# Routing the last two token tiles of a mixture-of-experts block: VectorE's steps in a hand-written order, and unread products on TensorE

## The chip, the cores and the metric

The kernel runs on one core of a Trainium2 chip. The metric is the device time of one execution in microseconds (us), as the median of several runs. A profile of one execution shows when each instruction of the five engines ran: TensorE (PE, with its weight loads as PEld), VectorE (DVE), ScalarE (ACT), GpSimd (POOL) and SyncE (SP, which issues transfers).

## What is computed

One layer of a streaming encoder for 1024 tokens of width 1024: a token mixer (attention and pooling branches, gated, then a projection `w_out`), a layer norm, and a mixture of experts with two-stage routing.

```
x = layer_norm(ALPHA * x + mix, ln1_gain, ln1_bias)
g_prob = softmax(x2 @ w_router_group + b_router_group)      # 4 groups
g_p, g_idx = top_k(g_prob, 1)
e_logit = (x2 @ w_router_expert + b_router_expert)          # 8 experts of the chosen group
e_p, e_local = top_k(softmax(e_logit), 2)
weights = g_p * e_p / sum(e_p)
...
yb = (silu(gate) * up) @ w_down[e]        # for the tokens of each of 32 experts
out = segment_sum(yb * row_w, row_tok)
x = layer_norm(ALPHA * x + ffn, ln2_gain, ln2_bias)
```

## The kernel before

Tokens are worked in eight tiles of 128 behind the mixer. The projection by `w_out` goes in groups of tiles, (0, 1), 2, 3, 4, 5 and (6, 7). For each tile `residual` adds the input and `norm` does the layer norm (L788 to L798), and then the tile goes through five steps, called by `step`:

- `turn` (L813, L814): TensorE transposes the tile x in two groups of four pieces, and ScalarE copies each group into the tile xT.
- `y` (L949): ScalarE writes ALPHA times x, which POOL stores.
- `route`: `logits` multiplies xT by the router's weights (L820, 16 products of 36 columns with their weight loads), VectorE adds the bias (L822, tile lg), and then some twenty small VectorE instructions of 4 or 32 columns (L829 to L857) pick the group G, the first and the second expert (oh), their masks M, and the sum of the masks, Ms. ScalarE has one exponential in it (L832).
- `weights` (L865 to L874): the two weights of the token. VectorE forms the negative of the first maximum (L869), ScalarE takes an exponential (L870), and VectorE makes the weights of it.
- `places` (L879 to L891): TensorE counts with `tri`, `one` and the running count `cum` how many earlier tokens chose the same expert, and VectorE makes one-hot rows (tile ohr) out of it by comparing (L890).
- `place` (L898, L899): TensorE multiplies the one-hot rows, which puts tokens and weights into the table `first`; VectorE adds it, and L903 and L905 make the entries of an overflow table.

While later tiles are projected, the steps of the earlier ones run beside them. Tiles 6 and 7 have nothing beside them: the list `S5_END` names their steps in order, behind the last projection. When the last `place` is done, `rows_at` (L1017, L1018) turns `first` into row numbers, POOL gathers the rows of the first experts (L1093), TensorE transposes them (L1033, tile X), ScalarE and VectorE split them in two parts (L147, L148), and the first expert's products begin (tile gu, three products L162, L163, L164 for each piece). 32 experts follow.

In the stage before the experts, PE and ACT carry out their instructions in the order of the program text, within a stretch that a `manual_schedule` context marks; VectorE's order is chosen by a scheduler, from estimated times. Each engine works its queue strictly in order, so an instruction that waits holds up all behind it.

Of the kernel before, what the change touches and what calls it, by code (L numbers as in the profile page):

```python
# [11 lines left out]
F32 = mybir.dt.float32  # L12
F32R = mybir.dt.float32r
BF = mybir.dt.bfloat16
# [11 lines left out]
NE = 32  # L26

CAP = 96
# [35 lines left out]
    5: ((3, "places", 3), (10, "turn", 4), (10, "place", 3), (12, "route", 4)),  # L64
    7: ((3, "places", 4), (10, "turn", 5), (10, "place", 4), (12, "route", 5), (21, "places", 5), (26, "place", 5)) + S5_LATE,
}
S5_END = (("y", 6), ("logits", 6), ("route", 6), ("turn", 7), ("y", 7), ("weights", 6), ("logits", 7), ("route", 7), ("places", 6), ("weights", 7), ("place", 6), ("places", 7), ("place", 7))
Y_OUT = (6, 7)
COMB = ()
M4 = 4  # L70
# [36 lines left out]
def body(tc, ctx, A, out):  # L107
# [26 lines left out]
    def st(shape, name="st", dt=F32):  # L134
        return sm.tile([128] + shape, dt, name=nm(name), tag="st", bufs=8)
# [4 lines left out]
    def tiny(shape, name, dt=F32, bufs=2):  # L140
        return (ph["S2"] if "S2" in ph else sm).tile([128] + shape, dt, name=nm(name), tag="t_" + name, bufs=bufs)
# [675 lines left out]
    def logits(xT1):  # L817
        pr = p5.tile([128, 512], F32, name=nm("pr"), tag="R", bufs=2)
        for k in range(8):
            PE.matmul(pr[:, :36], xT1[:, k], wr[:, k], start=k == 0, stop=k == 7)  # L820
        lg = tiny([36], "lg")
        DVE.tensor_add(lg, pr[:, :36], br)  # L822
        return lg, pr

    def route(j, lg, pr):

        s = tiny([16], "s")
        gm, ngm, sg = (s[:, i:i + 1] for i in range(3))
        DVE.tensor_reduce(gm, lg[:, 0:4], AX.X, OP.max)  # L829
        DVE.tensor_scalar(ngm, gm, -1.0, None, op0=OP.mult)  # L830
        eg, G = tiny([4], "eg"), tiny([4], "G")
        ACT.activation(eg, lg[:, 0:4], AF.Exp, bias=ngm, accum_out=sg)  # L832

        le, to = lg[:, 4:36].rearrange("p (g e) -> p g e", g=4), lambda v: v[:, :, None].to_broadcast([128, 4, 8])
        mx, f, oh, t = tiny([2, 4], "mx"), tiny([2, 4], "f"), tiny([2, 4, 8], "oh"), tiny([2, 4, 8], "t", bufs=1)
        tg, fg = tiny([4], "tg"), tiny([1], "fg")
        DVE.tensor_reduce(mx[:, 0], le, AX.X, OP.max)
        DVE.scalar_tensor_tensor(tg, lg[:, 0:4], gm, down8[:, :4], op0=OP.is_equal, op1=OP.mult)
        for k in range(2):
            v = t[:, k]  # L840
            DVE.tensor_tensor(v, le, to(mx[:, k]), op=OP.is_equal)
            DVE.tensor_mul(v, v, down8[:, None, :].to_broadcast([128, 4, 8]))
            if k == 0:
                DVE.tensor_reduce(fg, tg, AX.X, OP.max)
                DVE.tensor_scalar(G, tg, fg, None, op0=OP.is_equal)
            DVE.tensor_reduce(f[:, k], v, AX.X, OP.max)
            DVE.tensor_tensor(oh[:, k], v, to(f[:, k]), op=OP.is_equal)
            if k == 0:
                big = tiny([4, 8], "big", bufs=1)
                DVE.scalar_tensor_tensor(big, oh[:, 0], NEG, le, op0=OP.mult, op1=OP.add)  # L850
                le = big
                DVE.tensor_reduce(mx[:, 1], le, AX.X, OP.max)
        M = tiny([2, NE], "M")
        for k in range(2):
            DVE.tensor_tensor(M[:, k].rearrange("p (g e) -> p g e", g=4), to(G), oh[:, k], op=OP.mult)
        Ms = tiny([NE], "Ms", BF)
        DVE.tensor_add(Ms, M[:, 0], M[:, 1])  # L857
        return M, Ms, pr, s, mx, G, eg

    def weights(j, s, mx, G, eg):  # L860

        gm, ngm, sg, me, gp, m1, m2, nm1, e2, w = (s[:, i:i + 1] for i in range(10))
        eq = tiny([2, 4], "eq", bufs=1)
        for k, m in enumerate((m1, m2)):
            DVE.scalar_tensor_tensor(eq[:, k], mx[:, k], 1.0, G, op0=OP.mult, op1=OP.mult, accum_out=m)  # L865
        DVE.tensor_reduce(me, eg, AX.X, OP.max)
        DVE.reciprocal(sg, sg)
        DVE.tensor_mul(gp, me, sg)
        DVE.tensor_scalar(nm1, m1, -1.0, None, op0=OP.mult)  # L869
        ACT.activation(e2, m2, AF.Exp, bias=nm1)  # L870
        DVE.tensor_scalar(w, e2, 1.0, None, op0=OP.add)
        DVE.reciprocal(w, w)
        DVE.tensor_mul(pay[:, j, 0, 2:3], w, gp)
        DVE.tensor_mul(pay[:, j, 1, 2:3], pay[:, j, 0, 2:3], e2)  # L874

    def places(j, M, Ms, pr):

        pp = pr[:, 256:288]
        PE.matmul(pp, tri, Ms, start=True, stop=False)  # L879
        PE.matmul(pp, one, cum, start=False, stop=True)  # L880
        oh = st([2, CAP + 2 * NE], "ohr")
        at = tiny([2], "at")
        for k in range(2):
            DVE.tensor_scalar(oh[:, k, CAP:CAP + NE], M[:, k], pay[:, j, 0, 3:4], None, op0=OP.mult)
            DVE.tensor_scalar(oh[:, k, CAP + NE:], M[:, k], pay[:, j, k, 2:3], None, op0=OP.mult)
        for k in range(2):
            t = tiny([NE], "pt", bufs=1)
            DVE.scalar_tensor_tensor(t, M[:, k], 1.0, pp, op0=OP.mult, op1=OP.mult, accum_out=at[:, k:k + 1])
        for k in range(2):
            DVE.tensor_scalar(oh[:, k, :CAP], slots, at[:, k:k + 1], None, op0=OP.is_equal)  # L890
        DVE.tensor_add(cum, cum, Ms)  # L891
        return M, pr, oh, at

    def place(j, M, pr, oh, at):

        pf = pr[:CAP, 384:448]
        for k in range(2):
            PE.matmul(pf, oh[:, k, :CAP], oh[:, k, CAP:], start=k == 0, stop=k == 1)  # L898
        DVE.tensor_add(first, first, pf.rearrange("p (c e) -> p c e", c=2))  # L899
        sf = tiny([2], "sf")  # L900
        for k in range(2):
            t = tiny([NE], "pt", bufs=1)
            DVE.scalar_tensor_tensor(t, M[:, k], float(ROWS), cst[:, C_IOTA:C_IOTA + NE], op0=OP.mult, op1=OP.mult,  # L903
                                     accum_out=sf[:, k:k + 1])
        DVE.tensor_add(entry[:, j], sf, at)  # L905

    def store_rows(j):
        for k in range(2):
            q = POOL.indirect_dma_start(out=TAB, out_offset=IO(ap=entry[:, j, k:k + 1], axis=0), in_=pay[:, j, k], in_offset=None,
                                        bounds_check=NE * ROWS - 1, oob_is_err=False)  # L910
            for o in scat:
                tc.declare_no_dep(q.ins, o.ins, reason="other rows of the table")
            scat.append(q)
# [25 lines left out]
    def step(what, j):  # L939

        if what == "turn":
            x = tl[j]["x"]
            tl[j]["t"] = turned(x)
            if j not in Y_OUT:
                POOL.tensor_scalar(x, x, ALPHA, None, op0=OP.mult)
                POOL.dma_start(Y[j * 128:j * 128 + 128], x)
        elif what == "y":
            y = slot2([D], F32, "yy")
            ACT.activation(y, tl[j]["x"], AF.Copy, scale=ALPHA)  # L949
            POOL.dma_start(Y[j * 128:j * 128 + 128], y)  # L950
        elif what == "route":
            if "l" not in tl[j]:
                tl[j]["l"] = logits(tl[j]["t"])
            tl[j]["m"] = route(j, *tl[j]["l"])
            if j < 6:
                weights(j, *tl[j]["m"][3:])
        elif what == "logits":
            tl[j]["l"] = logits(tl[j]["t"])
        elif what == "weights":
            weights(j, *tl[j]["m"][3:])  # L960
        elif what == "places":
            tl[j]["p"] = places(j, *tl[j]["m"][:3])
        else:
            place(j, *tl[j]["p"])
            if j < 6:
                store_rows(j)


    with tc.manual_schedule(engines={mybir.EngineType.PE, mybir.EngineType.Activation}):
        for group in ((0, 1), (2,), (3,), (4,), (5,), (6, 7)):  # L970
            for j in group:
                begin(j)
            todo = list(S5[group[-1]])
            i = 0
            for n in range(2):
                for j in group:
                    for k in range(8):
                        while todo and todo[0][0] <= i:
                            step(*todo.pop(0)[1:])
                        mix(j, k, n)  # L980
                        i += 1
                    if i == 32:
                        for s_ in todo:
                            step(*s_[1:])
                    residual(j, n)
                    if n:
                        norm(j)
        for what, j in S5_END:
            step(what, j)
    ps5.__exit__(None, None, None)  # L990
    s2.__exit__(None, None, None)
    smp.__exit__(None, None, None)
# [427 lines left out]
```

## Time and profile before

| what | value |
|---|---|
| median of 3 runs | 1561.75 us (1561.41 to 1564.54) |
| profiled execution, own time | 1562.51 us |
| its span, first to last instruction | 1560.7 us |
| TensorE busy | 1486.8 us, 95% of the span |
| VectorE busy | 1192.4 us, 76% |
| ScalarE busy | 947.6 us, 61% |
| last projection product starts, first expert product starts | 922.48 us, 947.18 us |

Times in rows of the trace are counted from the start of the span. In a timeline row stand start, duration, engine, line, operation, the tiles written and read, and in brackets how long the engine was idle just before and what ended the wait. Instructions of an engine overlap a little, so distances of starts say more than durations.

### The profile page before, as it was taken

What the parts mean: (1) busy time and instruction counts of PE and PEld (TensorE: products, weight loads), DVE (VectorE), ACT (ScalarE), POOL (GpSimd) and SP (SyncE); (2) the same over time, 40 slices, a digit from 0 to 9 for tenths busy, and PEclk for the clock granted to TensorE, in tenths of its full rate; (3) what the DMA queues carried; (4) which work ended last, traced back from release to release, by engine and by line L of the source; (5) the groups of instructions that cost most, each with busy time, mean ns of one, the idle gap of its engine ahead of it and who ended that gap; (6) DMA issues with size and microseconds to landing.
All of it is one profiled execution on the core that took longest, in us unless ns stands there. A gap on an engine that the chain in (4) does not pass through costs nothing.

```text
span 1560.7 us, 22003 instructions
## 1 busy us (share of the span) xinstructions
PE 1486.8 (95%) x7627; PEld 1188.4 (76%) x7627; DVE 1192.4 (76%) x2284; ACT 947.6 (61%) x1573; POOL 270.3 (17%) x229
## 2 busy tenths in 40 slices
PE   8999999999999999999999988999999999999980
PEld 6988887798798898888887875777777777776750
DVE  5774214987988987775565778999989999898967
ACT  4323124665666666775341126888888888888864
POOL 0001000220211211100002524222222222211410
PEclk9999999999999999999999998999999999999995
DMA  7156223746856755628465577999999999999945
GB/s 237 58 173 202 81 74 102 222 150 169 229 189 175 215 182 145 155 68 303 149 255 209 180 264 267 384 374 376 375 379 358 363 366 358 358 354 371 397 140 215
DMA packets 116977, 375.46 MB, mean 241 GB/s; under 512 B 13767, under 2 KB 44871, under 8 KB 91504
## 3 DMA queue, kind: packets, MB, share of 16 engines
q1 hardware_dynamic: 76128, 303.25, 52.9%
q0 software_dynamic: 40160, 69.96, 17.2%
q8 instruction: 61, 1.00, 0.3%
q10 hardware_dynamic: 576, 0.83, 0.2%
q14 instruction: 52, 0.43, 0.1%
HBM read 312.44 MB, written 69.78 MB: 245 GB/s over the span
## 4 chain that ended last, share of the span: by engine, by line
PE 55%; issue 28%; POOL 9%; DVE 5%; ACT 2%; DMA 1%; POOLq 0%; DVEq 0%; SPq 0%; ACTq 0%
POOL Y L1105 7%; PE ps L570 4%; PE pg L162 4%; PE pg L163 4%; PE pg L164 4%; PE po L621 3%; PE pv L162 2%; PE pv L164 2%; PE pv L163 2%; POOL xg L1093 2%; PE pa L164 2%; PE pa L163 2%; PE pa L162 2%; PE tp L606 2%; PE pw L162 2%
## 5 line engine op out<-in xcount | busy, mean ns | idle before, releaser
L148 DVE TENSOR_TENSOR wh<-we,wh 128x1024 fp32r<-128x1024 f32 x384 | 459.8, 1219 | 52.8 <-ACT wh L147 49.3
L147 ACT CAST wh<-we 128x1024 fp32r<-128x1024 f32 x384 | 400.6, 1047 | 88.5 <-PE gu L164 50.9
L162 PE MATMUL gu<-wh,xT 128*96 128x512 f32 x512 | 203.8, 398 | 0.0
L164 PE MATMUL gu<-wh,xT 128*96 128x512 f32 x512 | 202.2, 395 | 0.5 <-DVE xT L148 0.5
L163 PE MATMUL gu<-wh,xT 128*96 128x512 f32 x512 | 201.3, 393 | 0.0
L1105 POOL DMA_INDIRECT Y<-y,idx x32 | 108.7, 3398 | 265.1 <-ACT y L1113 260.3
L148 DVE TENSOR_TENSOR w<-wraw,w 128x512 fp32r<-128x512 f32 x111 | 75.7, 686 | 93.3 <-ACT w L147 92.9
L147 ACT CAST w<-wraw 128x512 fp32r<-128x512 f32 x111 | 68.5, 621 | 116.0 <-PE pg L164 36.4
L573 ACT ACTIVATE P<-ps,stat 128x256 f32<-128x256 f32 (+7 forms) x128 | 94.9, 742 | 59.0 <-DVE stat L572 58.6
L164 PEld LDWEIGHTS gu<-wh,xT 128*96 128x96 f32 x512 | 82.7, 162 | 36.8 <-DVE xT L148 1.1
L163 PEld LDWEIGHTS gu<-wh,xT 128*96 128x96 f32 x512 | 83.1, 162 | 33.9
L162 PEld LDWEIGHTS gu<-wh,xT 128*96 128x96 f32 x512 | 82.8, 162 | 33.0 <-ACT xT L147 0.2
L162 PE MATMUL dn<-wh,hT 128*96 128x512 f32 x256 | 102.4, 400 | 0.6 <-ACT hT L147 0.6
L570 PE MATMUL ps<-K,Q 128*128 128x512 f32 (+2 forms) x384 | 99.6, 364 | 1.2 <-DVE z L461 0.8
L164 PE MATMUL dn<-wh,hT 128*96 128x512 f32 x256 | 100.7, 393 | 0.0
L163 PE MATMUL dn<-wh,hT 128*96 128x512 f32 x256 | 100.6, 393 | 0.0
L162 PE MATMUL pg<-xT,w 128*128 128x512 f32 x256 | 100.4, 392 | 0.0
L163 PE MATMUL pg<-xT,w 128*128 128x512 f32 x256 | 100.0, 391 | 0.0
L164 PE MATMUL pg<-xT,w 128*128 128x512 f32 x256 | 99.9, 390 | 0.0
L572 DVE TENSOR_REDUCE stat<-ps 128x1 f32<-128x256 f32 (+7 forms) x128 | 95.4, 747 | 1.1
L570 PEld LDWEIGHTS ps<-K,Q 128*128 128x128 f32 x384 | 64.6, 189 | 10.8 <-DVE z L461 1.3
L162 PE MATMUL pv<-w,xT 128*128 128x256 f32 x256 | 72.8, 284 | 0.0
(277 smaller groups left out, 3382.4 us busy)
## 6 DMA issues: line engine op xcount, KB each, us to landing
we<-in_we_dram SPq DMA_DIRECT2D x192, 1024.0 KB, 22.8
wraw<-in_w_dram SPq DMA_DIRECT2D x61, 512.0 KB, 3.8
Q<-RQ POOLq DMA_DIRECT2D x64, 256.0 KB, 5.2
RQ<-rh SPq DMA_DIRECT2D x32, 256.0 KB, 3.3
K<-RK POOLq DMA_DIRECT2D x16, 512.0 KB, 5.2
V<-RV POOLq DMA_DIRECT2D x16, 512.0 KB, 5.5
OT<-ohl SPq DMA_DIRECT2D x48, 128.0 KB, 2.6
oT<-OT POOLq DMA_DIRECT2D x6, 1024.0 KB, 11.6
```

Of the source, the lines that this page charges most:

```text
L147: ACT.copy(hi, src)
L148: DVE.tensor_sub(lo, src, r(hi))
L162: PE.matmul(ps, a[0], b[0], start=start, stop=False)
L163: PE.matmul(ps, a[0], b[1], start=False, stop=False)
L164: PE.matmul(ps, a[1], b[0], start=False, stop=stop)
L570: PE.matmul(ps[:, c:c + n], q[:, o, m, qc], Kt[h, m][:, c:c + n], start=o == 0, stop=o == 1)
L572: DVE.tensor_reduce(st_[:, m:m + 1], ps[:, :W], AX.X, OP.max, negate=True)
L573: ACT.activation(Pt[h, i][m][:, :W], ps[:, :W], AF.Exp, bias=st_[:, m:m + 1], accum_out=st_[:, 2 + m:3 + m])
L606: PE.transpose(ps[:, k], p[:, (4 * g + k) * 128:(4 * g + k) * 128 + 128], ident)
L621: PE.matmul(o[:, 0, c], Vt[h][:, a, kt], aT[kt // 4][:, kt % 4, b, c], start=j == 0, stop=j == len(parts) - 1)
L1093: q = POOL.indirect_dma_start(out=x, out_offset=None, in_=X1, in_offset=IO(ap=idx[:, int(e < NXG), expert[e]:expert[e] + 1], axis=0), boun ...
L1105: q = POOL.indirect_dma_start(out=Y, out_offset=IO(ap=idx[:, 0, expert[e]:expert[e] + 1], axis=0), in_=y, in_offset=None, bounds_check=T - ...
```

## The change

The list `S5_END` goes, and a function `last_two` takes its place, in a context in which VectorE's order too is that of the program text. To write that order, `route`, `weights`, `places` and the new `onehots` and `entries` become generators: each `yield` ends a single VectorE step, and `some`, `by_turns` and `all_of` run so many steps of one, alternate two, or run all. Within `weights`, the negative (now L882) and the exponential (L883) come before the reciprocals. `place` is split into TensorE's part and VectorE's (`placed`). `idle(n)` issues n products of the constants `one` and `tri` (128 x 128, bf16) into a PSUM tile that nobody reads. For the six earlier tiles the same functions run without interleaving. Removed lines of the generators that only moved are left out here.

```diff
-S5_END = (("y", 6), ("logits", 6), ("route", 6), ("turn", 7), ("y", 7), ("weights", 6), ("logits", 7), ("route", 7), ("places", 6), ("weights", 7), ("place", 6), ("places", 7), ("place", 7))
...
+    def all_of(*steps):
+        for g in steps:
+            for _ in g:
+                pass
+
+    def by_turns(g, h):
+
+        for _ in h:
+            next(g, None)
+
+    def some(g, n):
+        for _ in range(n):
+            next(g, None)
...
+    def idle(n):
+
+        ps = p5.tile([128, 512], F32, name=nm("pw"), tag="W", bufs=4)
+        for i in range(n):
+            PE.matmul(ps[:, :128], one, tri, start=True, stop=True)
+
+    def last_two():
+
+        step("y", 6)
+        tl[6]["l"] = logits(tl[6]["t"])
+        r = route(6)
+        some(r, 12)
+        by_turns(r, weights(6))
+        all_of(r)
+        idle(32)
+        step("turn", 7)
+        step("y", 7)
+        all_of(onehots(6, 0), onehots(6, 1))
+        tl[7]["l"] = logits(tl[7]["t"])
+        r = route(7)
+        some(r, 2)
+        by_turns(r, places(6))
+        idle(16)
+        place(6)
+        idle(20)
+        by_turns(r, entries(6))
+        some(r, 2)
+        w = weights(7)
+        for _ in range(7):
+            some(w, 1)
+            some(r, 1)
+        all_of(r)
+        p = places(7)
+        placed(6)
+        all_of(onehots(7, 0), w, onehots(7, 1), p)
+        idle(18)
+        place(7)
+        all_of(entries(7))
+        placed(7)
+        idle(96)
...
-        for what, j in S5_END:
-            step(what, j)
+    with tc.manual_schedule(engines={mybir.EngineType.PE, mybir.EngineType.Activation, mybir.EngineType.DVE}):
+        last_two()
```

The first place where instructions move is VectorE's queue at the logits of tile 7. Tiles with numbers from 9393 to 9423 are those of tile 6 here, lg_9462 and what is made of it belong to tile 7. Before:

```order
L842 TENSOR_TENSOR t_9402<-t_9402,cst 128x32
L846 TENSOR_REDUCE f_9400<-t_9402 128x4
L822 TENSOR_TENSOR lg_9462<-pr_9453,br 128x36
L847 TENSOR_TENSOR oh_9401<-t_9402,f_9400 128x32
L829 TENSOR_REDUCE s_9464<-lg_9462 128x1
L837 TENSOR_REDUCE mx_9470<-lg_9462 128x4
L855 TENSOR_TENSOR M_9420<-G_9397,oh_9401 128x32
L830 TENSOR_SCALAR s_9464<-s_9464 128x1
L838 SCALAR_TENSOR_TENSOR tg_9474<-lg_9462,s_9464,cst 128x4
L857 TENSOR_TENSOR Ms_9423<-M_9420 128x32
L871 TENSOR_SCALAR s_9393<-s_9393 128x1
```

And in the changed kernel, where tiles 9396 to 9489 belong to tile 6, and lg_9503 and what is made of it to tile 7:

```order
L868 TENSOR_TENSOR M_9410<-G_9400,oh_9404 128x32
L891 TENSOR_SCALAR s_9396<-s_9396 128x1
L871 TENSOR_TENSOR Ms_9435<-M_9410 128x32
L893 RECIPROCAL s_9396<-s_9396 128x1
L895 TENSOR_TENSOR cst<-s_9396 128x1
L897 TENSOR_TENSOR cst<-cst,s_9396 128x1
L907 TENSOR_SCALAR ohr_9489<-M_9410,cst 128x32 x4
L821 TENSOR_TENSOR lg_9503<-pr_9494,br 128x36
L829 TENSOR_REDUCE s_9505<-lg_9503 128x1
L831 TENSOR_SCALAR s_9505<-s_9505 128x1
L919 SCALAR_TENSOR_TENSOR pt_9514,at_9513<-M_9410,pr_9385 128x32
L839 TENSOR_REDUCE mx_9516<-lg_9503 128x4
```

All of tile 6's route and weights, and four one-hot instructions, now stand ahead of the bias addition of tile 7; before, the second expert's mask (L847) and all behind it stood after it.

The second place is ScalarE's queue behind tile 6's first exponential. Before:

```order
L949 ACTIVATE yy_9379<-xx_9092 128x1024
L832 ACTIVATE eg_9396,s_9393<-lg_9391,s_9393 128x4
L814 COPY xT_9425<-px_9426 128x512
L814 COPY xT_9425<-px_9432 128x512
L949 ACTIVATE yy_9438<-xx_9097 128x1024
L870 ACTIVATE s_9393<-s_9393 128x1
```

And in the changed kernel:

```order
L833 ACTIVATE eg_9399,s_9396<-lg_9394,s_9396 128x4
L883 ACTIVATE s_9396<-s_9396 128x1
L813 COPY xT_9473<-px_9474 128x512
L813 COPY xT_9473<-px_9480 128x512
L1005 ACTIVATE yy_9486<-xx_9097 128x1024
```

The exponential of tile 6's weights (L870, now L883) moves from behind the two copies of tile 7's transposes to ahead of them; the large ScalarE instruction yy of tile 6 moves to ahead of tile 6's own copies.

## Rows read from the trace of the kernel before

**Rows 1.** Page, its head.

```profile
span 1560.7 us, 22003 instructions
```

**Rows 2.** Waits of TensorE in the experts' stage, 950 to 1520 us.

```profile
PE dn L162 <- ACT hT L147: 0.6, 1, 0.6
```

**Rows 3.** Windows: stretch, length, busy PE, PEld, DVE, ACT, POOL; clock; DMA, GB/s.

```profile
922.70:926.00 3.30, 3.02 (x25) 2.66 (x23) 2.98 (x7) 2.25 (x5) 0.59 (x1) 1.00 0.82 276
...
927.80:932.80 5.00, 4.89 (x24) 4.52 (x25) 2.28 (x20) 2.31 (x4) 1.07 (x2) 0.59 1.00 406
932.80:940.50 7.70, 2.19 (x12) 1.67 (x11) 7.18 (x76) 3.25 (x7) 0.00 (x0) 0.50 0.26 107
...
945.70:949.20 3.50, 3.49 (x13) 2.63 (x14) 1.70 (x3) 0.96 (x2) 2.89 (x3) 0.51 0.98 355
```

**Rows 4.** Timeline of TensorE, 920 to 950 us: start, duration, instructions, idle before.

```profile
923.99 1.98 PE L820 MATMUL pr<-wr,xT 128*128 128x36 f32 x16 [0.24 <-ACT xT L814]
927.84 1.62 PE L813 MATMUL px<-cst,xx 128*128 128x128 f32 x8 [1.88 <-DVE xx L798]
929.26 3.52 PE L820 MATMUL pr<-wr,xT 128*128 128x36 f32 x16
...
938.86 0.90 PE L898 MATMUL pr<-ohr 128*96 128x64 f32 x4 [1.75 <-DVE ohr L890]
945.71 1.54 PE L1033 MATMUL X<-cst,xg 96*128 96x96 f32 x8 [5.95 <-DMA xg<-X,idx]
947.18 0.74 PE L162 MATMUL gu<-wh,xT 128*96 128x512 f32 x1
...
948.14 0.63 PE L164 MATMUL gu<-wh,xT 128*96 128x512 f32 x1
948.57 0.63 PE L162 MATMUL gu<-wh,xT 128*96 128x512 f32 x1
...
949.54 0.39 PE L162 MATMUL gu<-wh,xT 128*96 128x512 f32 x1
```

**Rows 5.** Timeline of VectorE, 928 to 941 us.

```profile
928.28 0.18 DVE L842 TENSOR_TENSOR t<-t,cst 128x32 f32<-128x32 f32 x1
...
929.49 0.18 DVE L841 TENSOR_TENSOR t<-big,mx 128x32 f32<-128x32 f32 x1
...
929.71 0.19 DVE L842 TENSOR_TENSOR t<-t,cst 128x32 f32<-128x32 f32 x1
...
932.81 0.20 DVE L822 TENSOR_TENSOR lg<-pr,br 128x36 f32<-128x36 f32 x1 [2.69 <-PE pr L820]
...
936.67 0.17 DVE L857 TENSOR_TENSOR Ms<-M 128x32 bf16<-128x32 f32 x1
...
938.55 0.44 DVE L890 TENSOR_SCALAR ohr<-cst,at 128x96 f32<-128x96 f32 x2
...
939.80 0.22 DVE L899 TENSOR_TENSOR first<-first,pr 96x64 f32<-96x64 f32 x1 [0.47 <-PE pr L898]
```

**Rows 6.** Timeline of ScalarE, 924 to 932.5 us.

```profile
928.51 0.59 ACT L814 COPY xT<-px 128x512 f32<-128x512 f32 x1 [1.47 <-PE px L813]
929.50 0.59 ACT L814 COPY xT<-px 128x512 f32<-128x512 f32 x1 [0.41 <-PE px L813]
...
930.94 0.28 ACT L870 ACTIVATE s<-s 128x1 f32<-128x1 f32 x1
```

**Rows 7.** Timeline of POOL, 940 to 948 us.

```profile
941.34 1.30 POOL L1093 DMA_INDIRECT xg<-X,idx  x1 [9.47 <-DVE idx L1018]
```

**Rows 8.** Timeline of TensorE in the projection, 913.8 to 915 us.

```profile
913.82 0.40 PE L162 MATMUL pw<-wo,mg 128*128 128x512 f32 x1
914.05 0.39 PE L163 MATMUL pw<-wo,mg 128*128 128x512 f32 x1
...
914.52 0.19 PE L879 MATMUL pr<-Ms,tri 128*128 128x32 bf16 x1
914.55 0.18 PE L880 MATMUL pr<-cum,one 128*128 128x32 bf16 x1
```

More of the change, by code (lines that the diff above doesn't have):

```diff
@@ L823, in logits, with route @@
         return lg, pr
-    def route(j, lg, pr):
+    def route(j):
+        lg, pr = tl[j]["l"]
         s = tiny([16], "s")
@@ L829, in route @@
         DVE.tensor_reduce(gm, lg[:, 0:4], AX.X, OP.max)
+        yield
         DVE.tensor_scalar(ngm, gm, -1.0, None, op0=OP.mult)
@@ L832, in route @@
         ACT.activation(eg, lg[:, 0:4], AF.Exp, bias=ngm, accum_out=sg)
+        yield
         le, to = lg[:, 4:36].rearrange("p (g e) -> p g e", g=4), lambda v: v[:, :, None].to_broadcast([128, 4, 8])
@@ L837, in route @@
         DVE.tensor_reduce(mx[:, 0], le, AX.X, OP.max)
+        yield
         DVE.scalar_tensor_tensor(tg, lg[:, 0:4], gm, down8[:, :4], op0=OP.is_equal, op1=OP.mult)
+        yield
+        M = tiny([2, NE], "M")
+        tl[j]["m"] = M, s, mx, G, eg
         for k in range(2):
@@ L841, in route @@
             DVE.tensor_tensor(v, le, to(mx[:, k]), op=OP.is_equal)
-            DVE.tensor_mul(v, v, down8[:, None, :].to_broadcast([128, 4, 8]))
+            yield
             if k == 0:
                 DVE.tensor_reduce(fg, tg, AX.X, OP.max)
+                yield
+            DVE.tensor_mul(v, v, down8[:, None, :].to_broadcast([128, 4, 8]))
+            yield
+            if k == 0:
                 DVE.tensor_scalar(G, tg, fg, None, op0=OP.is_equal)
+                yield
             DVE.tensor_reduce(f[:, k], v, AX.X, OP.max)
+            yield
             DVE.tensor_tensor(oh[:, k], v, to(f[:, k]), op=OP.is_equal)
+            yield
             if k == 0:
@@ L850, in route, with weights @@
                 DVE.scalar_tensor_tensor(big, oh[:, 0], NEG, le, op0=OP.mult, op1=OP.add)
+                yield
                 le = big
                 DVE.tensor_reduce(mx[:, 1], le, AX.X, OP.max)
-        M = tiny([2, NE], "M")
-        for k in range(2):
+                yield
             DVE.tensor_tensor(M[:, k].rearrange("p (g e) -> p g e", g=4), to(G), oh[:, k], op=OP.mult)
-        Ms = tiny([NE], "Ms", BF)
+            yield
+        Ms = tl[j]["Ms"] = tiny([NE], "Ms", BF)
         DVE.tensor_add(Ms, M[:, 0], M[:, 1])
-        return M, Ms, pr, s, mx, G, eg
-    def weights(j, s, mx, G, eg):
+        yield
+    def weights(j):
+        M, s, mx, G, eg = tl[j]["m"]
         gm, ngm, sg, me, gp, m1, m2, nm1, e2, w = (s[:, i:i + 1] for i in range(10))
@@ L865, in weights, with onehots, places @@
             DVE.scalar_tensor_tensor(eq[:, k], mx[:, k], 1.0, G, op0=OP.mult, op1=OP.mult, accum_out=m)
-        DVE.tensor_reduce(me, eg, AX.X, OP.max)
-        DVE.reciprocal(sg, sg)
-        DVE.tensor_mul(gp, me, sg)
+            yield
         DVE.tensor_scalar(nm1, m1, -1.0, None, op0=OP.mult)
         ACT.activation(e2, m2, AF.Exp, bias=nm1)
+        yield
+        DVE.tensor_reduce(me, eg, AX.X, OP.max)
+        yield
+        DVE.reciprocal(sg, sg)
+        yield
+        DVE.tensor_mul(gp, me, sg)
+        yield
         DVE.tensor_scalar(w, e2, 1.0, None, op0=OP.add)
+        yield
         DVE.reciprocal(w, w)
+        yield
         DVE.tensor_mul(pay[:, j, 0, 2:3], w, gp)
+        yield
         DVE.tensor_mul(pay[:, j, 1, 2:3], pay[:, j, 0, 2:3], e2)
-    def places(j, M, Ms, pr):
+        yield
+    def onehots(j, what):
+        M = tl[j]["m"][0]
+        if what == 0:
+            tl[j]["oh"] = st([2, CAP + 2 * NE], "ohr")
+        oh = tl[j]["oh"]
+        for k in range(2):
+            DVE.tensor_scalar(oh[:, k, CAP + NE * what:CAP + NE * what + NE], M[:, k], pay[:, j, k * what, 3 - what:4 - what], None, op0=OP.mult)
+            yield
+    def places(j):
+        M, Ms, pr, oh = tl[j]["m"][0], tl[j]["Ms"], tl[j]["l"][1], tl[j]["oh"]
         pp = pr[:, 256:288]
@@ L880, in places @@
         PE.matmul(pp, one, cum, start=False, stop=True)
[L881 to L885, printed above, removed]
+        at = tl[j]["at"] = tiny([2], "at")
         for k in range(2):
@@ L888, in places, with entries @@
             DVE.scalar_tensor_tensor(t, M[:, k], 1.0, pp, op0=OP.mult, op1=OP.mult, accum_out=at[:, k:k + 1])
+            yield
         for k in range(2):
             DVE.tensor_scalar(oh[:, k, :CAP], slots, at[:, k:k + 1], None, op0=OP.is_equal)
+            yield
         DVE.tensor_add(cum, cum, Ms)
[L892 to L899, printed above, removed]
+        yield
+    def entries(j):
+        M, at = tl[j]["m"][0], tl[j]["at"]
         sf = tiny([2], "sf")
@@ L904, in place, with placed @@
                                      accum_out=sf[:, k:k + 1])
+            yield
         DVE.tensor_add(entry[:, j], sf, at)
+        yield
+    def place(j):
+        pf, oh = tl[j]["l"][1][:CAP, 384:448], tl[j]["oh"]
+        for k in range(2):
+            PE.matmul(pf, oh[:, k, :CAP], oh[:, k, CAP:], start=k == 0, stop=k == 1)
+    def placed(j):
+        pf = tl[j]["l"][1][:CAP, 384:448]
+        DVE.tensor_add(first, first, pf.rearrange("p (c e) -> p c e", c=2))
+    def all_of(*steps):
[8 more added lines that the diff above has]
+            next(g, None)
     def store_rows(j):
@@ L951, in step @@
         elif what == "route":
[L952 to L957, printed above, removed]
             tl[j]["l"] = logits(tl[j]["t"])
-        elif what == "weights":
-            weights(j, *tl[j]["m"][3:])
+            all_of(route(j), weights(j))
         elif what == "places":
-            tl[j]["p"] = places(j, *tl[j]["m"][:3])
+            all_of(onehots(j, 0), onehots(j, 1), places(j))
         else:
-            place(j, *tl[j]["p"])
-            if j < 6:
-                store_rows(j)
+            place(j)
+            placed(j)
+            all_of(entries(j))
+            store_rows(j)
+    def idle(n):
[35 more added lines that the diff above has]
+        idle(96)
     with tc.manual_schedule(engines={mybir.EngineType.PE, mybir.EngineType.Activation}):
```

## The prediction

> **What bounds the kernel now.** I read the span first [rows 1], then the waits of TensorE in the experts' stage, then a table of windows around the place that changes, then the engines' timelines there. In the experts' stage TensorE, from 950 to 1520 us, waits for nothing longer than 0.6 us [rows 2]; it sets the pace to its last product. So whatever brings the first expert product forward shortens the kernel by as much, and whatever delays it costs as much. The change must be judged by that one start, 947.18 us [rows 4].
>
> Behind the projection comes a chain with little beside it. The reader should see four links. TensorE stands idle 1.88 us before tile 7's transposes [rows 4]. The logits of tile 7 then take 3.52 us, where tile 6's took 1.98 us [rows 4]: the granted clock is 1.00 up to 926 us, and 0.59 on average from 927.8 to 932.8 us, that is, it fell to the lower level (1.2 GHz) in there, and it stays there at 0.50 and 0.51 until the experts have begun [rows 3]. VectorE waits 2.69 us for these logits at L822, and has tile 6's second choice still to do [rows 5]. From there it is busy 7.18 of 7.70 us [rows 3], until POOL's gather at 941.34 us [rows 7], whose rows arrive at 945.71 us, when TensorE begins the transposes [rows 4].
>
> **Start of tile 7's logits: no gain.** The transposes of tile 7 find ScalarE free before, and the first copy stands at 928.51, the second at 929.50 us [rows 6]. In the new queue tile 6's exponential (L883) is ahead of them, and needs the second maximum of tile 6. From the product with the descending numbers at 928.28 us five dependent VectorE steps lead there (reduction, compare, mask, maximum, weighted sum), and one such step is 0.22 us, the distance of L841 and L842 of one tile [rows 5]; a compare and the negative stand between or behind, and the negative ends near 929.8 us. The exponential takes 0.28 us [rows 6], so the first copy runs from 930.15 and the second ends near 931.3 us instead of 930.1. With TensorE at the full level the logits take 1.98 us, from 930.7 to 932.7 us; at the lower level 3.52 us, to 934.3 us. Before, the bias addition began at 932.81 us [rows 5]. What the clock wins the exponential takes back: I take 932.8 us, which is **0**, and keep +1.5 us as the other end. The 32 unread products fill the wait from 926 to 928.3 us or so; the copies hide them.
>
> **VectorE behind the logits: little.** Seven short instructions of tile 6 and three one-hot rows leave the busy stretch, but tile 7's own steps depend on each other, and the change puts others between them. I walked the new order, with 0.22 us for a dependent step and for independent ones the distances of starts in the same timeline, 0.07 to 0.18 us. From the bias addition at 0: maximum per group at 0.6, first compare 1.1, product 1.55, reduction 2.0 (each of these links doubled by tile 6's instructions), then mask 2.2, 2.45, second maximum 2.65, compare 3.0, and three steps on to M at 3.9; Ms at 4.1 us. Before, Ms came at 936.67, which is 3.86 us after [rows 5]. Then follow tile 6's table addition, two one-hot rows, reciprocal and two products in a chain, two more one-hot rows (to 5.3 us), two sums, and the last two compares end at 6.05 us. Before, they ended at 938.99 us, 6.18 us after [rows 5]. **Gain 0.1 us**, with 0.4 us of doubt both ways. What is queued behind the closing compares, the three entries of the overflow table, now stands ahead of the table addition, but ends while TensorE multiplies.
>
> **Table products of tile 7.** They took 0.90 us at the lower level [rows 4]. By then 16, 20 and 18 unread products have run, and I expect the full level: half, 0.45 us. **Together with the line above −0.5 us**: the table addition falls at 939.3 instead of 939.80 us [rows 5], the gather lands at 945.2 us.
>
> **The closing 96 products.** They start at 939.2 us and TensorE cannot begin the transposes before they are through. The trace has no stream of such products, so bounds: a column costs 0.23 us / 512 = 0.45 ns at the full level, from two products of 512 columns, which makes 58 ns for 128 columns [rows 8]. Two bf16 products of 32 columns with their loads start 0.03 us apart [rows 8], 16 ns more than their columns. So 58 to 74 ns; at the lower level 0.43 us / 512 [rows 4] makes 107 ns. I take 74 ns, because each product here has its load too: 7.1 us, to 946.3 us. That is 1.1 us after the gather's landing, and 0.6 us later than the transposes began before: **+0.6 us**. At 58 ns (5.6 us) the products end ahead of the landing, and the start gains 0.5 us.
>
> The Trainium skill, in TensorE: Matmul & The Clock Gate, section Back-to-back issue gap, gives about 81 ns for a 128-column product in a stream with weight loads. By that the 96 would be an estimate of 7.8 us, 0.7 us more than in my sum, and the change would be worth nothing; no row here shows such a stream.
>
> **First transposes and products at the full level.** From the first transpose to the first expert product 1.47 us pass, and the eight transposes take 1.54 us [rows 4]; the first four, half of them, stand ahead of the first copy and halve at the full level: 0.4 us less. The six steps from 947.18 to 949.54 us take 2.36 us [rows 4]; at 0.23 us each [rows 8] they take 1.39 us: 0.97 us less. **−1.4 us.**
>
> **The sum**: the 0.5 us are inside the start of the 96 products, so what counts is +0.6 for the transposes' start, −0.4 and −0.97, together −0.8 us at the first expert products, and at the end. The profiled execution took 1562.5 us, 1.8 us more than its span, and would take 1561.7. It stands 0.8 us above the median of the runs, 1561.75, from which I forecast **1561.0 us**. A measurement of this kernel tells a change from none at about 0.2%, 3.1 us: faster is below 1558.6, slower above 1564.9.
>
> The other steps cost nothing: tile 6's yy ahead of its own copies moves them from 923.4 to 923.5 us, which delays the bias addition of tile 6 by 0.1 us. The queues of POOL and SP keep their order. For tiles 0 to 5 VectorE's new order lies beside the projection, on which TensorE does not wait.
>
> **The rivals.**
> *The exponential does not hold the copies, and the unread products are cheap.* If tile 6's second maximum is there when the transposes end, the logits run at the full level from 929.2 to 931.2 us, 1.6 us earlier; with −0.5 for the table, with 58 ns and no overrun, and −1.4 for the clock, −3.5 us: 1558.3 us. For it speaks the wait of 2.69 us [rows 5], which looks like room; against it the order of ScalarE's queue.
> *The closing products overrun at the lower level.* If the clock does not rise on the earlier unread products, the logits end at 934.3, the table at 941.3 us, and 96 products at 107 ns take 10.3 us: transposes at 951.6, 5.9 us later than before, −1.4 at the full level: 1566.2 us. It turns at an end of the 96 products at 947.1 us, 1.4 us past the old start of the transposes; then the change loses. [...]
> *It does nothing.* Overrun and clock cancel, as at 81 ns: 1561.75 us.
>
> **How the numbers follow.** The forecast has 0.60: two of its terms are walked from rows, and its own range is from 1559.9 (58 ns) to 1562.5 us (logits at the lower level, +1.5). The first rival has 0.18, the second 0.14, the third 0.08. The range reaches to 1558.2, which takes in the first rival, and above to 1564.4 us, which takes in half an overrun and leaves the second rival out. Faster by over 0.2%: the first rival and a little, 0.19. Slower: the second, 0.14. Within: 0.67.
>
> **What would show it.** In the changed profile: the copies of tile 7 at 930 us, right behind the exponential; its bias addition near 932.8 us with VectorE idle before it; Ms 4.1 us and the last compare 6.05 us after that; the table products in 0.45 us; the 96 products in 7 us, ending behind the gather's landing, so that the transposes wait for TensorE's own queue and not for the gather; the clock at 1.00 from 940 us, and the first expert products 0.23 us apart. I am wrong if the copies come at 928.5 us, if the bias addition moves by over 1 us, or if the unread products take over 100 ns.

## The result and the profile after

The changed kernel is slower: 1585.63 us (median of 6 runs, 1582.95 to 1588.43) against 1562.27 us for the kernel before (6 runs, 1561.41 to 1566.22), a ratio of 1.0145 with a 95% interval of 1.0131 to 1.0158. The profiled execution took 1585.51 us. Its page begins:

```profile
span 1583.7 us, 22364 instructions
```

The span is 23.0 us longer than before [rows 1]. The timeline of TensorE from the last transposes of tile 6 on, in the changed kernel (columns as in [rows 4]):

```profile
923.51 1.03 PE L812 MATMUL px<-cst,xx 128*128 128x128 f32 x8
...
926.70 1.95 PE L1022 MATMUL pw<-tri,one 128*128 128x128 bf16 x32
...
931.61 2.52 PE L819 MATMUL pr<-wr,xT 128*128 128x36 f32 x16 [1.51 <-ACT xT L813]
...
940.28 0.56 PE L943 MATMUL pr<-ohr 128*96 128x64 f32 x4
940.68 5.52 PE L1022 MATMUL pw<-tri,one 128*128 128x128 bf16 x96
951.62 1.51 PE L1124 MATMUL X<-cst,xg 96*128 96x96 f32 x8 [5.41 <-DMA xg<-X,idx]
953.06 0.74 PE L161 MATMUL gu<-wh,xT 128*96 128x512 f32 x1
...
1537.31 0.39 PE L163 MATMUL dn<-wh,hT 128*96 128x512 f32 x1
```

Two rows of the kernel before, from the same view, give the starts that are compared:

```profile
922.71 1.04 PE L813 MATMUL px<-cst,xx 128*128 128x128 f32 x8
...
1514.46 0.39 PE L164 MATMUL dn<-wh,hT 128*96 128x512 f32 x1
```

Tile 6's transposes start 0.80 us later than before, and the first expert product 5.88 us later (953.06 against 947.18 [rows 4]). From the one to the other it is 29.55 us instead of 24.47: this stretch, the one that was changed, lost 5.1 us. The last product starts 22.85 us later; so the other 17.0 us are lost inside the experts' stage, in which the change touches nothing.

The gather is issued 1.15 us later than before [rows 7], and from there to TensorE's first transpose of its rows 9.13 us pass instead of 4.37. TensorE has been done with its 96 unread products since about 946.2 us, waits 5.41 us, and starts the transposes and the expert products at the lower clock level, 1.51 us for eight transposes as before. POOL's row:

```profile
942.49 1.30 POOL L1184 DMA_INDIRECT xg<-X,idx  x1 [8.66 <-DVE idx L1109]
```

A slow transfer asks what else the DMA engines moved. Windows of the kernel before (columns as in [rows 3]): 50 us near the end of the projection, the six microseconds ahead of the gather, and 100 us of the experts' stage:

```profile
870.00:920.00 50.00, 49.37 (x267) 41.10 (x266) 38.02 (x215) 7.27 (x23) 23.45 (x22) 1.00 0.56 199
...
935.00:941.00 6.00, 1.98 (x10) 1.56 (x10) 5.49 (x56) 3.36 (x6) 0.00 (x0) 0.50 0.04 16
...
1200.00:1300.00 100.00, 100.00 (x478) 71.30 (x477) 91.21 (x92) 85.17 (x104) 23.15 (x12) 1.00 1.02 361
```

And of the changed kernel:

```profile
870.00:920.00 50.00, 49.43 (x266) 41.02 (x265) 38.10 (x220) 7.00 (x22) 23.83 (x22) 1.00 0.29 98
...
935.00:941.00 6.00, 6.00 (x63) 5.74 (x61) 5.76 (x56) 1.49 (x5) 0.00 (x0) 0.61 1.01 423
...
1100.00:1150.00 50.00, 50.00 (x241) 35.66 (x240) 45.93 (x47) 42.63 (x52) 12.26 (x6) 1.00 1.02 366
...
1200.00:1300.00 100.00, 96.86 (x451) 66.75 (x450) 85.26 (x86) 77.95 (x96) 20.53 (x11) 1.00 1.01 369
```

The reader should see a displaced transfer. During the projection the DMA share has halved; ahead of the gather it is 1.01 where it was 0.04; and in the experts' stage, from some point behind 1150 us on, TensorE is no longer busy in the whole window, though the DMA engines are as full as before. What moved is on the queue of SP, which issues the expert weights. Its loads of expert weights in the changed kernel, in the timeline from 800 to 940 us:

```profile
918.44 20.56 SPq L1143 DMA_DIRECT2D we<-in_we_dram  x13
```

And in the kernel before:

```profile
808.77 114.46 SPq L1052 DMA_DIRECT2D we<-in_we_dram  x16
```

The waits of that queue, 780 to 1000 us, in the changed kernel (line, waited for, us in total, times, longest):

```profile
SPq L1143 <- PE pw L163: 106.6, 1, 106.6
```

One load waits 106.6 us, and nothing is issued behind it. The order of the queue says which; before, the first weight loads are these (the number is that of the tile):

```
L1052 DMA we_9574<-in_we_dram 128x2048
...
L1052 DMA we_9598<-in_we_dram 128x2048
L1052 DMA we_9631<-in_we_dram 128x2048
L1052 DMA we_9633<-in_we_dram 128x2048
```

and after:

```
L1143 DMA we_9821<-in_we_dram 128x2048
L1143 DMA we_9764<-in_we_dram 128x2048
L1143 DMA we_9766<-in_we_dram 128x2048
...
L1143 DMA we_9788<-in_we_dram 128x2048
L1143 DMA we_9823<-in_we_dram 128x2048
```

Before, thirteen loads (tiles 9574 to 9598) and then the fourteenth, 9631. After, the fourteenth, 9821, stands ahead of the thirteen. There are 192 such loads, and the two queues differ in these first fourteen places alone. The fourteenth is the one piece among them that `M_AT` puts in another pool (`extra` instead of `slot`), in memory that the projection still reads up to 918 us. So thirteen prefetches wait behind the one whose buffer comes free last. Their own buffers were free at once or came free earlier: before, the queue waited for the projection 11 times, 30.2 us at the longest, and issued load by load in between:

```profile
SPq L1052 <- PE pw L164: 102.1, 11, 30.2
```

**Theory A:** the loss is the order of this queue. With the load in its place the change is worth about what the prediction's terms gave (−0.8 us). **Rivals:** the unread products or VectorE's order by hand cost the time, and the loads are late for another reason; or the late loads explain only the later first product, and the 17 us have a cause of their own. The kernel before, run again beside the experiments, took 1564.87 us (25 runs) beside the mended kernel, the load at the head, the kernel without products and the products alone, and 1564.11 us (23 runs) beside the other three; each ratio below is to the one or the other.

### The profile page after: what moved, and what is told of

Same layout as the page of the kernel before. It is cut to its first block, busy times and chain, and to the rows that moved or that the text cites. A ratio compares the mean times of both kernels' runs of the same rounds, so it can differ in the third digit from the quotient of the medians.

```text
span 1583.7 us, 22364 instructions
## 1 busy us (share of the span) xinstructions
PE 1505.9 (95%) x7809; PEld 1198.1 (76%) x7809; DVE 1194.4 (75%) x2284; ACT 942.4 (60%) x1573; POOL 257.2 (16%) x229
## 3 DMA queue, kind: packets, MB, share of 16 engines
q8 instruction: 62, 1.02, 0.3%
## 4 chain that ended last, share of the span: by engine, by line
PE 51%; issue 30%; POOL 8%; DVE 6%; DMA 2%; ACT 2%; POOLq 0%; DVEq 0%; SPq 0%; ACTq 0%
POOL Y L1196 5%; PE ps L569 4%; PE pg L161 4%; PE pg L162 4%; PE pg L163 4%; PE po L620 3%; POOL xg L1184 3%; PE pa L161 2%; PE pa L162 2%; PE pa L163 2%; PE pv L161 2%; PE pv L163 2%; PE pv L162 2%; PE tp L605 2%; PE pB L162 2%
## 5 line engine op out<-in xcount | busy, mean ns | idle before, releaser
L146 ACT CAST wh<-we 128x1024 fp32r<-128x1024 f32 x384 | 395.1, 1046 | 115.3 <-DMA we<-in_we_dram 53.7
L1196 POOL DMA_INDIRECT Y<-y,idx x32 | 85.5, 2671 | 313.5 <-ACT y L1204 308.7
```

Of the source, the lines that this page charges most:

```text
L146: ACT.copy(hi, src)
L1196: q = POOL.indirect_dma_start(out=Y, out_offset=IO(ap=idx[:, 0, expert[e]:expert[e] + 1], axis=0), in_=y, in_offset=None, bounds_check=T - ...
```

## Experiments

### The changed kernel with the loads in their order

Each weight load is kept behind the one before it, which gives the queue the order of the kernel before in all 192 places; nothing else is touched.

```diff
-    pieces = {}
+    pieces, loads = {}, []
...
-            q = SP.dma_start(w, A["we"][expert[e], c].rearrange("p (k n) -> p k n", k=4))
+            with tc.issue_after(loads[-1].ins) if loads else ExitStack():
+                q = SP.dma_start(w, A["we"][expert[e], c].rearrange("p (k n) -> p k n", k=4))
             tc.keep_in_program_order(q)
+            loads.append(q)
```

> The changed kernel with one thing put back: the load of the 14th weight piece (the one in the buffer M) is issued behind the 13 others again, as in the kernel before. Theory A, the load at the head of SyncE's queue costs the 23 us: about 1561.5 us (within 3 us of the kernel before), first expert product near 947 us, loads of weight pieces issued from 809 us on, TensorE never waiting over 1 us in the experts' stage. Theory B, the hand order and the unread products cost it: stays at 1580 to 1590 us.

Measured: 1563.73 us, ratio 0.9993 (0.9983 to 1.0002), −1.1 us by the ratio; no change that can be told. The loads start at 810.22 us. TensorE's timeline:

```profile
923.86 1.04 PE L812 MATMUL px<-cst,xx 128*128 128x128 f32 x8
...
931.96 2.62 PE L819 MATMUL pr<-wr,xT 128*128 128x36 f32 x16 [1.51 <-ACT xT L813]
...
934.47 1.87 PE L1022 MATMUL pw<-tri,one 128*128 128x128 bf16 x16
...
936.77 2.34 PE L1022 MATMUL pw<-tri,one 128*128 128x128 bf16 x20
...
941.13 5.52 PE L1022 MATMUL pw<-tri,one 128*128 128x128 bf16 x96
947.41 0.85 PE L1124 MATMUL X<-cst,xg 96*128 96x96 f32 x8 [0.75 <-DMA xg<-X,idx]
948.49 0.47 PE L161 MATMUL gu<-wh,xT 128*96 128x512 f32 x1 [0.24 <-ACT xT L146]
```

and its window ahead of the gather:

```profile
935.00:941.00 6.00, 5.91 (x60) 5.64 (x58) 5.79 (x56) 3.43 (x7) 0.00 (x0) 0.59 0.19 78
```

With a DMA share of 0.19 the gather, issued at 942.94 us, has landed by 947.41, 4.47 us later. The whole loss is gone, the 17 us in the experts' stage too (first to last expert product 567.02 us, before 567.28), with the unread products and VectorE's order still there. This is what Theory A says, and both rivals fall.

### The kernel before with the fourteenth load at the head

The other half of the proof: in the kernel before only this one load is issued first (`x` and `h` are allocated ahead of it, so that its buffer keeps its place; the loads are chained as above). All other instructions of every engine keep the order of the kernel before.

```diff
+            if i == 13:
+                pieces[e, c] = early
+                continue
...
+    x, h = turn_to(8, "xT"), rt([512], "h", F32, 1)
+    early = extra([4, 512], "we")
+    e, c = stream[13]
+    loads.append(SP.dma_start(early, A["we"][expert[e], c].rearrange("p (k n) -> p k n", k=4)))
+    tc.keep_in_program_order(loads[-1])
     ahead(13)
```

> The kernel before with one thing added: the load of the 14th weight piece is issued ahead of the 13 others. No step order and no product is changed. Theory A: 1580 to 1590 us, first weight load issued at 918 us and not at 809 us, first expert product near 952 us, TensorE waiting for split weights in the experts' stage. Theory B: 1562 us, as before.

Measured: 1584.65 us, ratio 1.0132 (1.0114 to 1.0149). The wait of SP's queue is there again:

```profile
SPq L1094 <- PE pw L164: 103.6, 1, 103.6
```

and TensorE waits for the rows without a single unread product in the kernel:

```profile
919.41 1.04 PE L813 MATMUL px<-cst,xx 128*128 128x128 f32 x8
...
947.59 1.54 PE L1033 MATMUL X<-cst,xg 96*128 96x96 f32 x8 [10.67 <-DMA xg<-X,idx]
949.06 0.74 PE L162 MATMUL gu<-wh,xT 128*96 128x512 f32 x1
```

Both parts of the loss are there: 29.65 us from tile 6's transposes to the first product (5.2 more than before), and 585.17 us from there to the last product at 1534.23 us (17.9 more). One moved load makes 1.32% of the 1.45%, with every other step as before; the two intervals overlap.

### Half of the dose

Are late rows and late weights one loss or two? Here six loads go ahead of the waiting one and seven stand behind it (`ahead(6)` before `early`).

> The kernel before, with the load of the 14th weight piece issued behind 6 others and ahead of 7. Theory A as a matter of amount: the late traffic counts, not the place. In e2_head_of_queue 14 pieces came late, 38 us of transfers at 2.75 us each, and 20 to 23 us were lost, so some 16 us are absorbed; here 8 pieces come late, 22 us, and 4 to 8 us are lost. If the place alone counted, 20 us are lost; if only the gather's contention with the weights counted, 5 us, and all of it ahead of the first expert product.

Measured: 1570.79 us, ratio 1.0047 (1.0032 to 1.0062), about +7 us. Its window, its gather on POOL, and the transposes:

```profile
935.00:941.00 6.00, 1.98 (x10) 1.56 (x10) 5.49 (x57) 1.43 (x3) 0.00 (x0) 0.50 1.03 430
```

```profile
941.46 1.30 POOL L1105 DMA_INDIRECT xg<-X,idx  x1 [9.63 <-DMA we<-in_we_dram]
```

```profile
951.20 1.54 PE L1033 MATMUL X<-cst,xg 96*128 96x96 f32 x8 [11.33 <-DMA xg<-X,idx]
952.67 0.74 PE L162 MATMUL gu<-wh,xT 128*96 128x512 f32 x1
```

From tile 6's transposes (922.36 us) to the first product it is 30.31 us, 5.84 more than before, as in the changed kernel; but in the experts' stage TensorE waits for nothing over 0.6 us, and that stage takes 568.85 us, 1.6 more than before, where it took 584.25 in the changed kernel. That kernel has these waits there (955 to 1540 us):

```profile
PE gu L163 <- DVE xT L147: 6.0, 15, 0.8
PE gu L162 <- DVE wh L147: 3.3, 7, 0.8
```

and on ScalarE, which splits the weights (955 to 1545 us; the kernel before has 9 waits of this kind, 8.1 us):

```profile
ACT wh L146 <- DMA we<-in_we_dram: 53.7, 52, 2.3
```

TensorE's waits add up to 9.3 us and not to 17. The rest shows as no idle time: a product of 512 columns is recorded with 0.39 or 0.40 us while the next starts 0.23 us behind it, so that a start can be up to some 0.16 us late without a wait. The counts show it: 451 products instead of 478 in the window from 1200 to 1300 us, which is 5.6 us of work, with 3.1 us of idle time.

So they are two losses. The gather beside late weights costs 5.1 to 5.8 us at the first product, with fourteen late pieces or eight; the time forecast here for an amount of late traffic (4 to 8 us) was met, but nearly all of it falls ahead of the first product, where the expectation had put the contention alone. Eight late pieces the experts' stage makes up; fourteen it does not, and TensorE then follows the transfers: the 17 us. They do not come at once. The changed kernel still keeps TensorE busy in the whole of 1100 to 1150 us, with the DMA engines full (share 1.02). That reads as a stock of weights loaded ahead that is used up little by little, since engines that are already full do not build it up again; this is argued from the windows and not shown by a run of its own.

### Without the unread products

The mended kernel without the 182 products (`idle` 32, 16, 20, 18, 96).

> The changed kernel with the load's place put back and without the 182 unread products: the hand order alone. If the products keep TensorE at the upper level, their absence costs 1.5 us at the logits of tile 7, 0.45 us at the table products and 1.4 us at the first expert's transposes and products, and gives back the closing products' end: about 2 us slower than e1_order_mended, 1563 us. If the products are worth nothing, both are equal. Theory B: over 1570 us, if the hand order is what costs.

Measured: 1564.97 us, ratio 1.0005 (0.9994 to 1.0015), 1.9 us above the mended kernel by the ratios.

```profile
928.71 3.63 PE L819 MATMUL pr<-wr,xT 128*128 128x36 f32 x16 [0.86 <-ACT xT L813]
...
945.44 1.54 PE L1119 MATMUL X<-cst,xg 96*128 96x96 f32 x8 [6.04 <-DMA xg<-X,idx]
```

The clock is at the lower level again in both places: logits 3.63 us instead of 2.62, transposes 1.54 instead of 0.85. In the traces it is 26.30 us from tile 6's transposes to the first product, against 24.63 in the mended kernel and 24.47 before: the order by hand, without the products, lengthens the stretch. The two intervals of the times overlap, so the 1.9 us is a size, not a verdict.

### The unread products alone

The kernel before with its own step order, the same kind of products put into `S5_END`, and the loads in order. VectorE's and ScalarE's queues keep the order of the kernel before.

```diff
+S5_END = (("y", 6), ("logits", 6), ("route", 6), ("idle", 32), ("turn", 7), ("y", 7), ("weights", 6), ("logits", 7), ("route", 7), ("idle", 16), ("places", 6), ("weights", 7), ("idle", 20), ("place", 6), ("idle", 4), ("places", 7), ("idle", 18), ("place", 7), ("idle", 96))
...
-            step(what, j)
+            idle(j) if what == "idle" else step(what, j)
```

> The kernel before, its own step order, with 32, 16, 24, 18 and 96 unread products in TensorE's waits, and the weight loads held in their order. If the products bring the clock to the upper level: the logits of tile 7 in 2.0 us instead of 3.5, table products halved, about 1559.5 us. If they stand in the way (the closing 96 end behind the gather's landing): 1562 to 1564 us. Theory B, with the products at fault: over 1570 us.

Measured: 1559.98 us, ratio 0.9967 (0.9956 to 0.9978): faster than both kernels.

```profile
920.88 1.04 PE L813 MATMUL px<-cst,xx 128*128 128x128 f32 x8
...
927.31 1.98 PE L820 MATMUL pr<-wr,xT 128*128 128x36 f32 x16
...
943.02 0.47 PE L162 MATMUL gu<-wh,xT 128*96 128x512 f32 x1 [0.24 <-ACT xT L147]
```

The logits follow the transposes with no wait and run in 1.98 us, since no exponential stands ahead of the copies. The stretch is 22.14 us, against 24.47 before and 24.63 in the mended kernel. So the order by hand loses what the products win. Of the 5.1 us that the ratio gives, the stretch explains 2.3 and the first six product steps, at the full level from the start, another 0.8; 2 us stay unexplained. In this trace tile 6's transposes, ahead of all that was changed, start 1.83 us earlier than before; over the nine traces that start lies anywhere from 919.41 to 923.86 us, so that a difference of this size in single traces says nothing of the change.

### The mended kernel with tile 7's copies first

The 32 products and `turn` of tile 7 are moved ahead of tile 6's `weights`, so that L883 comes behind the copies (the lines that keep the loads in order are left out here).

```diff
-        by_turns(r, weights(6))
-        all_of(r)
         idle(32)
         step("turn", 7)
+        by_turns(r, weights(6))
+        all_of(r)
```

> e1_order_mended with one more edit: tile 7's transposes and copies stand ahead of tile 6's weights in the program text, so that ScalarE's exponential of tile 6 no longer holds the copies. If the exponential was the hold: bias addition of tile 7 8.5 us after the first transpose of tile 6 (10.75 us in e1_order_mended, 8.5 in e4_products_only), logits in 2.0 us, 2.2 us faster than e1_order_mended, and so 3 us faster than the kernel before. If the hand order loses elsewhere to the scheduler's order, it stays 2 us or more behind e4_products_only, at the time of e1_order_mended.

Measured: 1562.01 us, ratio 0.9987 (0.9977 to 0.9997). The copies and the exponential on ScalarE:

```profile
929.38 1.25 ACT L813 COPY xT<-px 128x512 f32<-128x512 f32 x2 [1.57 <-PE px L812]
930.70 0.29 ACT L883 ACTIVATE s<-s 128x1 f32<-128x1 f32 x1
```

and the bias addition on VectorE:

```profile
932.10 0.67 DVE L907 TENSOR_SCALAR ohr<-M,cst 128x32 f32<-128x32 f32 x4
932.69 0.18 DVE L821 TENSOR_TENSOR lg<-pr,br 128x36 f32<-128x36 f32 x1
```

The logits now take 1.98 us from 930.02 us on, and the bias addition comes 9.27 us behind tile 6's transposes, instead of 10.75 in the mended kernel. It could come earlier: it has no idle time ahead of it, because tile 6's one-hot rows stand before it in VectorE's queue. The scheduler's order, with the products alone, has it at 8.45 us. The stretch is 23.29 us, 1.34 less than in the mended kernel and 1.15 more than with the products alone. By the ratios the moved copies give back about 1 us, of 2.2 forecast and of the 4 that lie between the mended kernel and the products alone; the interval overlaps the mended kernel's, so the time itself does not show the gain. The order by hand loses elsewhere too, as the expectation had it for that case.

### Without the closing 96

The products alone, without the last 96.

> e4_products_only without the closing 96 unread products. They keep the clock up until the gather lands; without them the first expert's transposes and products run at the lower level: 0.4 us and 1 us more, and up to 1 us more where the clock rises later: 1.5 to 2.5 us slower than e4_products_only. If the clock stays up or the closing products delayed the start: equal or faster.

Measured: 1560.18 us, ratio 0.9975 (0.9966 to 0.9984), 1.2 us above the run with them by the ratios, a little under the forecast; the intervals overlap.

```profile
943.23 1.52 PE L1040 MATMUL X<-cst,xg 96*128 96x96 f32 x8 [6.12 <-DMA xg<-X,idx]
```

Through 6.12 us of idle time the clock falls (0.50 from 941 to 947 us), and the transposes take 1.52 us again.

## Why the prediction was wrong

**The step that failed** is the sentence "The queues of POOL and SP keep their order." SP's queue did not: one load moved past thirteen others, and 106.6 us of waiting moved ahead of them. The whole loss follows: with the load back in its place the span is 1561.9 us instead of 1583.7, and the time cannot be told from the kernel before. Without the numbers of the tiles the queue reads the same before and after, since all fourteen loads look alike. Because of that sentence no rival had late weights in it, and the range ended 21 us short of the result. What would have shown it beforehand is the list of that queue with the numbers of the tiles, beside the 102.1 us that it waits for the projection: a queue that waits so long is not hidden whatever its order. The prediction also took TensorE's lack of waits in the experts' stage as a sign that TensorE alone sets the pace there. It did so only while weights stood ready: the share of the DMA engines in the same stage was 1.02, and in the changed kernel TensorE fell behind by 17 us at a share of 1.01.

The other steps can be read in the mended kernel, counted from the start of tile 6's transposes so that its later start falls out.

- **Exponential ahead of the copies, bias addition unchanged:** the mechanism was right. ScalarE waits 2.89 us for the negative, and the copies follow at once:

```profile
931.14 0.30 ACT L883 ACTIVATE s<-s 128x1 f32<-128x1 f32 x1 [2.89 <-DVE s L882]
931.34 1.05 ACT L813 COPY xT<-px 128x512 f32<-128x512 f32 x2
```

  The prediction had 930.15 us for the copies with the transposes at 922.71, which is 7.44 us behind them; it is 7.48. The logits took 2.62 us, neither the 1.98 taken nor the 3.52 of the other end: in its wait of 1.51 us for the copies, which the prediction's own times imply and which it left without products, TensorE had nothing to do, and the windows 931 to 934.5 and 934.5 to 938 us show the clock at 0.80 and then 0.50 (with the copies first, the same logits follow without a wait and take 1.98 us):

```profile
931.00:934.50 3.50, 2.54 (x19) 2.54 (x20) 2.15 (x18) 2.21 (x4) 0.53 (x1) 0.80 0.97 392
934.50:938.00 3.50, 3.50 (x35) 3.50 (x34) 3.25 (x33) 0.43 (x3) 0.00 (x0) 0.50 0.41 167
```

  So the bias addition comes 10.75 us behind the transposes instead of 10.10: +0.65 where 0 was taken.
- **VectorE behind the logits:** Ms at 4.18 us and the last compares' end at 6.25 us behind the bias addition, predicted 4.1 and 6.05. The walk with 0.22 us for a dependent step held within 0.2 us; the gain of 0.1 did not come (before, the last compares ended at 6.18 us).
- **Table products:** 0.56 us, predicted 0.45, before 0.90.
- **Closing 96 products:** mis-sized. 5.52 us is 57.5 ns each, the lower bound of 58 that the row of 512 columns gave, and not the 74 taken: the load of the next product adds nothing that can be seen in this row. So they end ahead of the gather's landing, and the transposes wait for the gather (0.75 us), not for TensorE's own queue as the prediction had it. The 81 ns that the Trainium skill gives (TensorE: Matmul & The Clock Gate, Back-to-back issue gap) do not hold here; the measurement decides. Behind tile 7's logits, at the lower level, the 16 and the 20 products took 117 ns each (1.87 and 2.34 us), more than the 100 ns that the prediction named as a sign of being wrong; they stood in waits, and the products behind them start within 0.1 us of their operands.
- **Start of the transposes:** 23.55 us behind tile 6's, before 23.00: +0.55. The prediction had +0.6, but by an overrun that did not happen, so the agreement is luck. The table addition, forecast 0.5 us earlier, comes 0.45 us later (17.54 us behind tile 6's transposes, before 17.09), because of the late bias addition; the rows take another 0.10 us longer.
- **Full level:** from transposes to first product 1.08 us instead of 1.47, −0.39 (predicted −0.4); the first six steps 1.61 instead of 2.36, −0.75 (predicted −0.97).

The sum of what was costed is −0.6 us at the first products where −0.8 was forecast. In the medians' ratio it is −1.1 us, with an interval from −2.7 to +0.3; in the two traces, counted from tile 6's transposes to the last expert product, it is −0.10 us (591.65 against 591.75), so that the gain at the first products is not seen at the end. Of the rivals, the first had the price of the products right and the exponential wrong; the second fell, since the clock was up again when the closing products ran; the third, no change, is what the mended kernel cannot be told from.

What stays open: why the fourteenth load came to the head. Every load is marked with `keep_in_program_order` in both programs, and the scheduler that sets the queue's order moved this one all the same; that the mark did not hold it is seen, not explained. Tied each to the one before it with `issue_after`, the loads keep their order.

## What to carry to other kernels

After an edit that changes a scheduler's input, compare every issue queue with its buffer numbers, prefetches far from the edit among them: identical shapes hide a swap. A load whose buffer is not yet free when it is issued belongs behind all whose buffers come free earlier, for it holds the queue as long as it waits; tie the order down where it matters. And a transfer that arrives late can be paid twice: where it is used, as with fourteen late pieces, and where it now meets others on the DMA engines, as with eight and with fourteen.

## What had not been expected of the hardware

A gather whose rows arrive in 4.4 to 4.5 us on quiet DMA engines (share 0.04 in the kernel before and 0.19 in the mended one, from 935 to 941 us) took 9.1 us in the changed kernel and 9.7 us with eight late pieces, beside weights that moved at 423 and 430 GB/s. And 96 products of 128 bf16 columns with their own loads followed each other at 57.5 ns and left the clock at the upper level through the 0.75 us of idle time behind them: the transposes took 0.85 us there, against 1.51 us in the changed kernel, behind an idle time of 5.41 us.
